# A gated product placed right behind each gate, the convolution's steps respread around it, and the last output weights split behind the last gates

## The chip, the cores and the metric

The kernel runs on one core of one Trainium2 chip. A core has five engines that work side by side, each through its own queue of instructions in a fixed order: TensorE (PE, matrix products; PEld is its weight load), VectorE (DVE), ScalarE (ACT), GpSimd (POOL) and SyncE (SP, which here only issues transfers). They wait for each other through semaphores. Data lies in the on-chip memory SBUF, products come out in PSUM, and everything else is in the device's main memory. The metric is the device time of one execution in microseconds (us), lower is better.

## The reference, cut to what matters

Two layers over 1024 latent tokens of 1024 channels. The change is in the first, even layer: one input projection feeds a convolution branch (A) and a recurrence branch (B); each is gated by a SiLU, and one output projection joins them.

```python
def even_mixer(h, h0, p):
    z = h @ p["w_in"]
    va, vg, ga, xb, gb = jnp.split(z, [...], axis=-1)
    y_a = conformer_conv(va, vg, p) * jax.nn.silu(ga)
    y_b, hT = rglru_branch(xb, p, h0, True)
    y_b = y_b * jax.nn.silu(gb)
    return jnp.concatenate([y_a, y_b], axis=-1) @ p["w_out"], hT
```

`conformer_conv` is `u = va * sigmoid(vg)`, a convolution over 31 neighbouring tokens for each channel on its own, a layer norm over the channels, and a SiLU. The second layer (a pooling mixer) and a final norm follow.

## The kernel before

Channels lie on the 128 partitions, so 1024 channels are 8 tiles (`KT = 8`) of 128 x 1024 tokens, treated in two halves of 512 tokens. A matrix product in full fp32 accuracy is made of three passes: each operand is split into a high part that TensorE takes as it is and a low part, the rest (`mm3_fixed`, line 565: high times high, high times low, low times high for each of 8 k-tiles, so 24 matmuls for one half and 48 for a tile).

Through most of the even layer the order of every engine's instructions is written by hand: `on` (line 549) issues each instruction behind the last one of its engine. The transfers on SyncE's queue are ordered by the scheduler at build time. What runs around the change:

- *Weights.* `raw_split` (584): ScalarE casts a loaded weight tile to its high part (`wh`), GpSimd subtracts to get the low part (`wl`). There are two buffers each for the raw, high and low tile. `gb_weights(j)` (885) does this for the gate's weights of tile j while j < 8, for the output projection's weights `wob` of tile j - 8 after that.
- *Gates.* `gb_product(j, w)` (891) is the product `h @ w_in` for the gate's tile j. Its two PSUM tiles come from a pool of four. `gb_silu(j)` (901) lets ScalarE apply the SiLU into two SBUF tiles `sb` out of a pool of four, so gate j's tiles wait for those of gate j - 2 to be used up.
- *Gated products.* `gated(n, between)` (1068): for each half, SyncE loads the recurrence's row from main memory (`yr`, two buffers), VectorE multiplies it with the gate (both in SBUF), ScalarE casts the result (`ybh`), GpSimd subtracts (`ybl`). These two are TensorE's operand of k-tile n in the output product. Behind each half stand `between` steps of the convolution.
- *Convolution.* `conv(j)` (617) gives VectorE's work on channel tile j in steps, mostly one multiply-add with its accumulator in PSUM. `fill(n)` (692) issues the next n steps, wherever they stand. `ln_sums` (662) adds a finished tile to the layer norm's sums. One step is longer: `edge_sum` and the sum of even and odd columns (both inputs in SBUF).
- *Output products.* In the loop at 1158, `wob` of tile m is multiplied with all eight `ybh`, `ybl` (48 matmuls). For m = 0 the first seven k-tiles of both halves stand first, then k-tile 7 of the first half, its eviction, k-tile 7 of the second half. `wob_evict` (1098) scales on ScalarE, adds the input on GpSimd and stores. After each m, `gb_weights(KT + m + 2)` prepares the weights after the next, and further steps of the convolution are placed.

Of the kernel before, what the change touches and what calls it, by code (L numbers as in the profile page):

```python
# [20 lines left out]
KT = D // P  # L21
# [35 lines left out]
def body(ctx, tc, xT, ctxT, cc, ccol, modT, modW, win, gw, wout, wu, grp, wg, wo1, small, edge, ident, outT):  # L57
# [24 lines left out]
    def ttile(name):  # L82
        return tpool.tile([P, H], F32, tag="t", name=name)
# [4 lines left out]
    def psum(name):  # L88
        return pm.tile([P, H], F32, tag="mm", name=name)


    def wide(name):
        return pc.tile([P, S], F32, tag="xb", name=name)
# [462 lines left out]
    def act(*args, **kw):  # L556
        return on("act", nc.scalar.activation, *args, **kw)

    def cast(dst, src):
        return on("act", nc.scalar.copy, dst, src)  # L560

    def gp(*args, **kw):
        return on("pool", nc.gpsimd.tensor_tensor, *args, **kw)

    def mm3_fixed(ps, w, xs, cols):
        hi, lo = w
        xh, xl = xs
        for k in range(KT):
            kc = slice(k * P, (k + 1) * P)
            on("pe", nc.tensor.matmul, ps, hi[:, kc], xh[k][:, cols], start=(k == 0), stop=False)  # L570
            on("pe", nc.tensor.matmul, ps, hi[:, kc], xl[k][:, cols], start=False, stop=False)
            on("pe", nc.tensor.matmul, ps, lo[:, kc], xh[k][:, cols], start=False, stop=(k == KT - 1))
            yield

    def all_of(steps):
        for _ in steps:
            pass

    def raw_load(src, name):
        raw = wpool.tile([P, D], F32, tag="wr", name=f"wr_{name}")  # L580
        nc.sync.dma_start(raw, src)
        return raw

    def raw_split(raw, name):
        hi = wpool.tile([P, D], F32R, tag="wh", name=f"wh_{name}")
        lo = wpool.tile([P, D], F32R, tag="wl", name=f"wl_{name}")
        cast(hi, raw)
        gp(out=lo, in0=raw, in1=hi.bitcast(F32), op=sub)
        return hi, lo
# [14 lines left out]
    def vec(f, **kw):  # L604
        return on("vec", f, **kw) if fixed[0] else f(**kw)
# [56 lines left out]
    def ln_sums():  # L662
        for j in range(summed[0], ended[0]):
            for h in range(2):
                first = us[0][:, HALF[h]] if j == 1 else lnacc[h][:, :H]
                vec(nc.vector.tensor_tensor, out=lnacc[h][:, :H], in0=first, in1=us[j][:, HALF[h]], op=add)
        summed[0] = max(summed[0], ended[0])
# [24 lines left out]
    def fill(n):  # L692
        while n > 0:
            try:
                next(going[0])
                n -= 1
            except StopIteration:
                if begun[0] >= whole_[0]:
                    return
                going[0] = conv(begun[0])  # L700
                begun[0] += 1

    with ExitStack() as actx:
# [178 lines left out]
        gws = {}  # L882


        def gb_weights(j):
            src, name = ((win[4 * KT + j], f"gb{j}") if j < KT else
                         (wout[j - KT, 1], f"wob{j - KT}") if j < 2 * KT else
                         (win[2 * KT + (0, KT // 2)[j - 2 * KT]], f"ga{(0, KT // 2)[j - 2 * KT]}"))
            gws[j] = raw_split(raw_load(src, name), name)

        def gb_product(j, w):
            if j == 4:
                gps[j] = (lambda t: [t[:, h] for h in HALF])(wide(f"gb{j}"))
            else:
                gps[j] = [psum(f"gb{j}_{h}") for h in range(2)]
            for h in range(2):
                all_of(mm3_fixed(gps[j][h], w, (hh, hl), HALF[h]))
# [3 lines left out]
        def gb_silu(j):  # L901
            sbs[j] = [ttile(f"sb{j}_{h}") for h in range(2)]
            for h in range(2):
                act(sbs[j][h], gps[j][h], AF.Silu)
# [32 lines left out]
    def d2tile(name, dt=F32):  # L937
        return d2pool.tile([P, S], dt, tag="d2", name=name)
# [5 lines left out]
    def vtile(name):  # L944
        return vpool.tile([P, H], F32, tag="v", name=name)
# [122 lines left out]
    def gated(n, between):  # L1068
        th, tl = d2tile(f"ybh{n}", F32R), d2tile(f"ybl{n}", F32R)
        for h in range(2):  # L1070
            y = vtile(f"yr{n}_{h}")
            nc.sync.dma_start(y, yb_raw[n][:, HALF[h]])
            v = sbs[n][h]
            vec(nc.vector.tensor_tensor, out=v, in0=y, in1=v, op=mult)
            cast(th[:, HALF[h]], v)
            gp(out=tl[:, HALF[h]], in0=v, in1=th[:, HALF[h]].bitcast(F32), op=sub)
            fill(between)
        bh.append(th)
        bl.append(tl)
# [4 lines left out]
    gb_weights(5)  # L1084
    gb_product(5, gws[5])
    gated(1, 3)
    for j in range(3, KT + 1):
        if j < KT:
            gb_silu(j)
        if 3 < j < KT:  # L1090
            gb_weights(j + 2)
        if 3 < j < KT - 2:
            gb_product(j + 2, gws[j + 2])
        gated(j - 1, (0, 0, 4, 5, 5, 5, 3, 0)[j - 1])
        ln_sums()


    def wob_evict(m, h):
# [781 lines left out]
```

## Time and profile before

| what | value |
|---|---|
| time, median of 3 runs (lowest to highest) | 1294.51 us (1293.93 to 1298.01) |
| the profiled execution: its time, its span | 1293.43 us, 1291.6 us |
| PE busy, share of the span | 1263.2 us, 98% |
| DVE | 1134.7 us, 88% |
| ACT | 647.6 us, 50% |
| POOL | 287.5 us, 22% |

The span runs from the first to the last instruction of the profiled execution; its time has 1.8 us around that. In a timeline a row is: start and length in us, engine, line of the kernel, operation, what is written and read by tile names, shape, how many (x), and in brackets the idle time before it with what ended it. Line 553 is the helper behind `on`, so instructions there are told apart by their tiles: `conv` and `u` are the convolution, `sb` the gated product (and the SiLU, on ACT), `ybh`/`ybl` its parts, `wh_`/`wl_` parts of weights, `gb` and `wob` the gate's and the output's products. A group of waits has the total, the number of times and the longest. A matmul's row is 0.39 us long, but the next one starts 0.227 us after it, since they overlap. On VectorE too the next instruction starts a little before the end of a row.

### The profile page before, as it was taken

Reading aid. Unit: us, or ns where it says so; the run is one execution under the profiler, and the core shown is the slowest. Engines: PE = TensorE matmul, PEld = TensorE weight load, DVE = VectorE, ACT = ScalarE, POOL = GpSimd, SP = SyncE. Lnnn points to the kernel's source line nnn. Section 1 sums busy time; section 2 is a strip of 40 time slices with the busy share of each in tenths; the row PEclk is TensorE's granted clock in tenths of the full one; section 3 lists DMA queues with packets and bytes.
Section 4 is the critical chain, followed back from the end, with each engine's and each line's share of the span. In section 5 each row is a group of like instructions: output and inputs, shape, how many; then the busy total and the mean of one; then the engine's idle time right before and its main releaser. Section 6 shows DMA issues by size and latency. Waiting matters only on the chain.

```text
span 1291.6 us, 16081 instructions
## 1 busy us (share of the span) xinstructions
PE 1263.2 (98%) x5804; PEld 1039.1 (80%) x5804; DVE 1134.7 (88%) x1761; ACT 647.6 (50%) x937; POOL 287.5 (22%) x146
## 2 busy tenths in 40 slices
PE   9999999999999999999999999999999999999995
PEld 7788888888888887888887878887877888788784
DVE  6899999999999999969869959998999987987775
ACT  8555566656656533237434347534333334645542
POOL 0003464436453466434200032000000000000002
PEclk9999999999999999999999999999999999999997
DMA  9951121112111234432418565333332334968623
GB/s 366 398 215 49 42 74 42 64 42 74 60 63 57 82 114 138 146 133 82 163 49 289 190 220 153 112 131 139 123 127 85 114 122 134 322 214 283 228 75 130
DMA packets 78783, 182.33 MB, mean 141 GB/s; under 512 B 7664, under 2 KB 23408, under 8 KB 78704
## 3 DMA queue, kind: packets, MB, share of 16 engines
q1 hardware_dynamic: 70256, 177.12, 39.5%
q10 hardware_dynamic: 8448, 4.20, 1.2%
q8 instruction: 45, 0.74, 0.2%
q14 instruction: 34, 0.28, 0.1%
HBM read 137.24 MB, written 44.04 MB: 140 GB/s over the span
## 4 chain that ended last, share of the span: by engine, by line
PE 48%; DVE 31%; DMA 13%; issue 4%; ACT 3%; POOL 1%; SPq 0%; POOLq 0%; DVEq 0%; ACTq 0%
DVE conv L553 7%; PE wob L553 6%; PE vg L553 5%; PE va L553 5%; PE xb L553 4%; PE fold L123 3%; DVE l L553 3%; PE g L553 3%; DVE ws L1417 2%; DMA wr_v<-wfold 2%; DMA yr_t<-y_t 2%; PE ga L553 2%; PE ga L146 2%; PE ga L145 2%; PE ga L144 2%
## 5 line engine op out<-in xcount | busy, mean ns | idle before, releaser
L553 DVE SCALAR_TENSOR_TENSOR conv<-u,sm,conv 128x505 f32<-128x505 f32 (+6 forms) x224 | 153.5, 746 | 1.0
L1699 POOL TENSOR_TENSOR o<-x,rr 128x256 f32<-128x256 f32 (+1 forms) x9 | 8.1, 929 | 454.3 <-ACT rr L1687 451.3
L553 ACT ACTIVATE l<-g,sm 128x512 f32<-128x512 f32 (+1 forms) x96 | 58.6, 618 | 57.8 <-PE g L553 57.0
L103 ACT CAST wq_g<-wr_g 128x512 fp32r<-128x512 f32 x48 | 28.2, 620 | 54.1 <-DMA wr_g<-wg 18.2
L123 PE MATMUL fold<-gh,wh_wu 128*128 128x512 f32 x128 | 51.1, 400 | 1.8 <-ACT wh_wu L103 1.8
L553 POOL TENSOR_TENSOR l<-l,l 128x1280 f32<-128x1280 f32 x16 | 47.1, 2966 | 25.6 <-DVE conv L553 14.1
L553 PE MATMUL wob<-ybl,wh_wob 128*128 128x512 f32 x128 | 50.3, 393 | 2.3 <-POOL ybl L553 2.3
L123 PE MATMUL fold<-gh,wl_wu 128*128 128x512 f32 x128 | 50.2, 395 | 0.5 <-DVE wl_wu L104 0.5
L553 PE MATMUL gb<-h0h,wl_gb 128*128 128x512 f32 x128 | 50.0, 391 | 0.4 <-POOL wl_gb L553 0.4
L123 PE MATMUL fold<-gl,wh_wu 128*128 128x512 f32 x128 | 50.2, 392 | 0.0
L103 ACT CAST wq_v<-wr_v 128x512 fp32r<-128x512 f32 x48 | 28.1, 620 | 44.1 <-DMA wr_v<-wfold 18.5
L553 PE MATMUL va<-h0h,wl_va 128*128 128x512 f32 x128 | 50.0, 390 | 0.1
L553 PE MATMUL vg<-h0h,wl_vg 128*128 128x512 f32 x128 | 50.0, 390 | 0.0
L553 PE MATMUL gb<-h0h,wh_gb 128*128 128x512 f32 x128 | 49.9, 390 | 0.0
L553 PE MATMUL wob<-ybh,wh_wob 128*128 128x512 f32 x128 | 49.9, 390 | 0.0
L553 PE MATMUL gb<-h0l,wh_gb 128*128 128x512 f32 x128 | 49.9, 390 | 0.0
L553 PE MATMUL va<-h0h,wh_va 128*128 128x512 f32 x128 | 49.9, 390 | 0.0
L553 PE MATMUL wob<-ybh,wl_wob 128*128 128x512 f32 x128 | 49.9, 390 | 0.0
L553 PE MATMUL vg<-h0l,wh_vg 128*128 128x512 f32 x128 | 49.9, 390 | 0.0
L553 PE MATMUL va<-h0l,wh_va 128*128 128x512 f32 x128 | 49.9, 390 | 0.0
L553 PE MATMUL vg<-h0h,wh_vg 128*128 128x512 f32 x128 | 49.9, 390 | 0.0
L553 DVE TENSOR_TENSOR_SCAN l<-l,l 128x256 f32<-128x256 f32 (+1 forms) x32 | 48.7, 1522 | 1.1
(593 smaller groups left out, 4290.2 us busy)
## 6 DMA issues: line engine op xcount, KB each, us to landing
wr_wu<-wu SPq DMA_DIRECT2D x16, 512.0 KB, 4.7
modw<-modW SPq DMA_DIRECT2D x16, 512.0 KB, 10.2
x_part<-xp SPq DMA_DIRECT2D x32, 256.0 KB, 2.2
mod<-modT SPq DMA_DIRECT2D x32, 256.0 KB, 3.9
wr_v<-wfold SPq DMA_DIRECT2D x16, 512.0 KB, 4.2
wr_g<-wg SPq DMA_DIRECT2D x16, 512.0 KB, 5.3
wr_wo<-wo SPq DMA_DIRECT2D x16, 512.0 KB, 4.4
yr_t<-y_t SPq DMA_DIRECT2D x16, 512.0 KB, 5.7
```

Source lines behind the costliest of these rows:

```text
L103: return (nc.scalar.copy(hi, src), eng.tensor_tensor(out=lo, in0=src, in1=hi.bitcast(F32), op=sub))
L123: m = nc.tensor.matmul(*args, **kw)
L144: mm(ps, hi[:, kc], xh[k][:, cols], start=(k == 0), stop=False)
L145: mm(ps, hi[:, kc], xl[k][:, cols], start=False, stop=False)
L146: mm(ps, lo[:, kc], xh[k][:, cols], start=False, stop=(k == ks - 1))
L553: last[eng] = f(*args, **kw)
L1417: nc.vector.tensor_tensor(out=nxt[:, :, a_:b_], in0=cur[:, :, a_ + o0 : b_ + o0], in1=cur[:, :, a_ + o1 : b_ + o1], op=add)
L1699: nc.gpsimd.tensor_tensor(out=o[:, k - k0], in0=v, in1=rr, op=mult)
```

## The change

Before, the loop for j issues the SiLU of gate j and then the gated product of gate j - 1, so each product stands one gate behind. After, the product of gate j follows the SiLU of gate j. The weights of the gates' tile 6 and the output weights are placed anew between them, and the numbers of convolution steps between the products are others: behind each half of gates 2 to 7 it was 4, 5, 5, 5, 3, 0, and is 2, 3, 5, 5, 5, 4. The weights of output product 1 (`gb_weights(KT + 1)`), which stood ahead of gate 6's product, come behind gate 7's.

```diff
     gb_weights(5)
     gb_product(5, gws[5])
     gated(1, 3)
-    for j in range(3, KT + 1):
-        if j < KT:
+    gb_silu(3)
+    gb_weights(6)
+    gated(2, 2)
+    gb_silu(4)
+    gb_product(6, gws[6])
+    for j in range(3, KT):
+        if j > 4:
             gb_silu(j)
-        if 3 < j < KT:
-            gb_weights(j + 2)
-        if 3 < j < KT - 2:
-            gb_product(j + 2, gws[j + 2])
-        gated(j - 1, (0, 0, 4, 5, 5, 5, 3, 0)[j - 1])
+        if j == 5:
+            gb_weights(7)
+            gb_product(7, gws[7])
+        elif j == 6:
+            gb_weights(KT)
+        gated(j, (3, 5, 5, 5, 4)[j - 3])
         ln_sums()
+    gb_weights(KT + 1)
```

On each engine the same instructions run in both kernels. TensorE's order is unchanged, and so is every order ahead of gate 2's product and behind the weights of output product 1, but for the two layer-norm sums of the next channel tile, which stand three steps earlier. On ScalarE and GpSimd, between those two points, the parts of the weights and of the gated products follow each other as the lines above say. On SyncE the weights' transfers change places with some of the rows' transfers.

## The prediction

> **What bounds the kernel now.** I read the busy table first, then who TensorE waited for around the changed lines, then the timelines of that stretch engine by engine.
>
> ```profile
> span 1291.6 us, 16081 instructions
> PE 1263.2 (98%) x5804; PEld 1039.1 (80%) x5804; DVE 1134.7 (88%) x1761; ACT 647.6 (50%) x937; POOL 287.5 (22%) x146
> ```
>
> TensorE sets the time: 28 us of the span are left to win in the whole kernel. The waits of PE between 420 and 680 us are two groups (total, times, longest), and the starts of four matmuls put a size to them:
>
> ```profile
> PE wob L553 <- POOL ybl L553: 2.3, 3, 1.6
> PE gb L553 <- POOL wl_gb L553: 0.4, 1, 0.4
> ```
> ```profile
> 473.49 0.39 PE L553 MATMUL gb<-h0h,wh_gb 128*128 128x512 f32 x1
> 485.15 0.39 PE L553 MATMUL gb<-h0h,wh_gb 128*128 128x512 f32 x1
> 496.03 0.39 PE L553 MATMUL wob<-ybh,wh_wob 128*128 128x512 f32 x1
> 510.11 0.40 PE L553 MATMUL wob<-ybh,wh_wob 128*128 128x512 f32 x1
> ```
>
> These are the first matmuls of gate product 6, gate product 7, output product 0 and output product 1, each of 48 matmuls. Product 7 runs clean: 496.03 - 485.15 = 10.88, or 0.227 a matmul. Product 6 takes 11.66 (0.78 lost to its low weights), output product 0 takes 14.08 (3.20 lost to the last gated rows). So the stretch can give back 3.98 us at most, 0.31% of the time. What follows it has no slack for PE to hide in:
>
> ```profile
> 496.00:521.00 25.00, 22.68 (x97) 17.80 (x96) 24.61 (x38) 6.90 (x10) 14.09 (x9) 1.00 0.41 138
> 521.00:587.00 66.00, 66.00 (x292) 54.64 (x291) 53.43 (x81) 22.13 (x32) 29.39 (x17) 1.00 0.39 133
> 587.00:677.00 90.00, 90.00 (x398) 74.54 (x398) 71.97 (x110) 48.62 (x74) 19.80 (x9) 1.00 0.30 99
> ```
>
> The second number of a row is PE's busy time: 66.00 of 66.00 and 90.00 of 90.00. When output product 1 starts later by some time, so does everything behind it, up to 677 us and, as the later chain starts from PE's products there, beyond.
>
> **The change part by part.** TensorE's own instruction order is the same in both kernels, and nothing is added or removed on any engine; only orders on VectorE, ScalarE, GpSimd and SyncE change, all between gate 2's product and output product 1. What decides is when the last gated product (gate 7, second half) ends on VectorE, and what GpSimd still has to do before output product 1.
>
> *The end of the chain.* Before, it runs so:
>
> ```profile
> 505.51 1.29 DVE L553 TENSOR_TENSOR sb<-yr,sb 128x512 f32<-128x512 f32 x2
> ```
> ```profile
> 470.97 1.04 ACT L553 CAST wh_gb<-wr_gb 128x1024 fp32r<-128x1024 f32 x1
> 506.23 1.23 ACT L553 CAST ybh<-sb 128x512 fp32r<-128x512 f32 x2 [4.67 <-DVE sb L553]
> ```
> ```profile
> 497.96 2.40 POOL L553 TENSOR_TENSOR wl_wob<-wr_wob,wh_wob 128x1024 fp32r<-128x1024 f32 x1 [2.41 <-ACT wh_wob L553]
> 506.93 2.54 POOL L553 TENSOR_TENSOR ybl<-sb,ybh 128x512 fp32r<-128x512 f32 x2 [3.66 <-ACT ybh L553]
> ```
>
> Call the end of the last gated product X: 505.51 + 1.29 = 506.80. The low part ends at 506.93 + 2.54 = 509.47 (it queues behind its sister half), and output product 1 starts at 510.11, X + 3.31. Its own low weights were made at 497.96, long before. After, `gb_weights(KT + 1)` stands behind the last gated row, so on ScalarE the weights' cast (1.04) follows the last cast, hidden by GpSimd's low part, and on GpSimd the 2.40 follow that low part. The two halves no longer stand back to back, so the low part ends at X + 0.62 + 1.29 + 0.1 of handing over = X + 2.0, the weights at X + 4.4. Output product 1 needs them at its third matmul, 0.45 after its start, and pays about 0.15 of slow first matmuls; that equals a start at X + 4.15. Against X + 3.31: **+0.85**. There is no cover for it, since PE has nothing else in its queue.
>
> *How X moves, the transfer.* Up to the last gated product VectorE has the same work in both orders, counted from gate 2's first half: 44 convolution steps, the two sums for the layer norm, the gated products. So X moves only by waits.
>
> ```profile
> 461.72 1.23 DVE L553 TENSOR_TENSOR sb<-yr,sb 128x512 f32<-128x512 f32 x1
> 462.87 2.71 DVE L553 SCALAR_TENSOR_TENSOR conv<-u,wsum,conv 128x509 f32<-128x509 f32 x4
> 466.76 1.65 DVE L553 TENSOR_TENSOR sb<-yr,sb 128x512 f32<-128x512 f32 x1 [1.18 <-DMA yr<-yb_raw]
> ```
> ```profile
> 462.42 0.33 SPq L581 DMA_DIRECT2D wr_gb<-win  x1
> 462.85 9.13 SPq L1072 DMA_DIRECT2D yr<-yb_raw  x4
> ```
>
> Gate 2's second half waits for its recurrence row, which SyncE issues behind gate 7's weights (512 KB); those wait for GpSimd to finish the low weights of gate 5. Both orders have the two transfers in this sequence, so the row lands at 466.7 again. The new order puts 2 steps instead of 4 (0.655 each, 2.71 for 4 overlapped) before that product: VectorE waits 1.18 + 1.31. **+1.3**; the steps it would have filled the time with come later, before X. Bounds: 0 if the row lands sooner, and +1.3 is also the most that two steps can be.
>
> *How X moves, the meetings with GpSimd.* A VectorE instruction with both inputs in SBUF takes longer when GpSimd is in an instruction of its own. Undisturbed lengths are the first three rows, the others are disturbed:
>
> ```profile
> 450.24 0.68 DVE L553 TENSOR_TENSOR sb<-yr,sb 128x512 f32<-128x512 f32 x1
> 453.69 0.15 DVE L553 SCALAR_TENSOR_TENSOR edge_junk<-u,sm 128x8 f32<-128x8 f32 x1
> 453.89 0.70 DVE L553 TENSOR_TENSOR u<-u 128x512 f32<-128x512 f32 x1
> ...
> 475.27 1.02 DVE L553 TENSOR_TENSOR sb<-yr,sb 128x512 f32<-128x512 f32 x1
> 484.55 0.87 DVE L553 TENSOR_TENSOR sb<-yr,sb 128x512 f32<-128x512 f32 x1
> 499.53 1.38 DVE L553 TENSOR_TENSOR sb<-yr,sb 128x512 f32<-128x512 f32 x1
> 500.83 1.22 DVE L553 SCALAR_TENSOR_TENSOR edge_junk<-u,sm 128x8 f32<-128x8 f32 x1
> 502.10 1.73 DVE L553 TENSOR_TENSOR u<-u 128x512 f32<-128x512 f32 x1
> ```
> ```profile
> 459.99 2.41 POOL L553 TENSOR_TENSOR wl_gb<-wr_gb,wh_gb 128x1024 fp32r<-128x1024 f32 x1 [1.70 <-ACT wh_gb L553]
> 466.58 1.28 POOL L553 TENSOR_TENSOR ybl<-sb,ybh 128x512 fp32r<-128x512 f32 x1 [1.22 <-ACT ybh L553]
> 480.02 3.59 POOL L553 TENSOR_TENSOR wl_gb<-wr_gb,wh_gb 128x1024 fp32r<-128x1024 f32 x1 [1.70 <-ACT wh_gb L553]
> ```
>
> The product at 461.72 ends when GpSimd's at 459.99 does (462.40) plus its own length, the one at 466.76 when the one at 466.58 does; at 480.02 GpSimd was the one to wait (3.59 for 2.40). Before, VectorE loses 0.55 + 0.97 + 0.34 + 0.19 + 0.70 + 1.07 + 1.03 = 4.9. For the new order I walked the queues from 461.72 on with these lengths. Gate 6's low weights now run right behind gate 1's low parts, 467.0 to 469.7: no wait for PE at 473.9, so the 0.78 is gone. But gate 3's first product comes at 468.7 and waits 0.9, its second 0.4, gate 4's first 0.75 behind gate 3's low part. Gate 7's weights now stand behind both rows of gate 4: 483.5 to 485.9. There the two layer-norm sums (484.2) wait 1.7, and PE waits about 1.1 for them (it wants them at 484.8). Output product 0's weights run 494.1 to 496.5, gate 6's first product waits 1.5; the sum of even and odd columns waits 1.0 once more, gate 2's first product its 0.55. That is 6.8: **+1.9**. Bounds: with no new meetings only 0.55 + 1.0 are left, -3.3; with three meetings of a full 2.40 and four of 1.29, 12.4, +7.5. I take the walk's value, as the same walk with the old order ends on X within 0.3 us of the trace.
>
> PE's new wait of 1.1 at gate 7 and the vanished waits cost and bring nothing by themselves: PE meets the chain of X again inside output product 0. That product would start near 496.5, reach the last rows' second half (46th matmul) near 507.5, and stand there some 3 us.
>
> *Sum:* 0.85 + 1.3 + 1.9 = +4.05, with X near 510.0 and output product 1 effectively at 514.15. The profiled execution took 1293.43 (span 1291.6 and 1.8 around it); it becomes 1297.5. The median of the runs, 1294.51, stands 1.08 above that execution, so the forecast is **1298.6**. The later convolution is covered:
>
> ```profile
> DVE ml_mu L553 <- ACT mh_mu L553: 10.0, 1, 10.0
> ```
>
> VectorE idles 10.0 there, ahead of the layer norm's mean, since ScalarE's part of it follows PE's products, which now come 4 later themselves; VectorE comes 3.2 later and still waits. Without this cover PE's mean matmuls would be late by what VectorE is.
>
> **The clock.** The granted clock stays 1.00 over the stretch (the windows' column before the last two) with a PE wait of 1.6 in it (the longest of the `wob` group). If it halved behind the wait of 3 us, each matmul would take 0.227 more; between no matmul and one whole product that is 0 to +10.9. I take 0, as the wait of 1.6 left it whole. The Trainium skill, "TensorE: Matmul & The Clock Gate", "What's actually happening", has the clock halve after an idle window of about 3.4 us and come back after as long a busy one; by it a gap a little longer than mine would cost, as an estimate from that page, 1.7 us more. No gap of the trace of before is long enough to try it.
>
> **The rivals.**
> - *Not slower: the meetings go away.* With products close behind their gates, GpSimd could be done with each low part before VectorE's next product. For it: GpSimd is busy only 14.09 of the 25.00 us of the first window above; against it: the weights' 2.40 now fall into the steps between products three times. Price: -3.3 + 1.3 + 0.85 = -1.15, or 1293.4. It decides once X is below 506.80 - 0.85, i.e. VectorE loses less than 2.8 to meetings. Chance 0.10; only near the ceiling of 3.98 (0.03 of it) would it show as faster by over 0.3%.
> - *The meetings sum up as before.* Then only 0.85 + 1.3 = +2.15 are left: 1296.7. Chance 0.18. A gain of PE elsewhere that takes up part of the shift looks the same from outside.
> - *Slower still.* The weights meet VectorE three times at full length (7.2 of the 12.4 in the bound, so +7.5 less some), or the clock drops behind the long gap: about +7, 1301.5. Chance 0.12.
> - *The change does not do what it says:* a product cannot stand right behind its gate where its row has not landed. For gate 2 that is so, at the +1.3 above, and is in the sum; for the others the rows are issued a whole product ahead (two buffers), so it has no chance of its own.
>
> **How the numbers follow.** The forecast has 0.60, its own range 1297.4 to 1300.6. What a measurement of this kernel can tell from no change is about 0.3%, 3.9 us: slower from 1298.4 on. A sixth of the forecast's chance lies under that, so slower is 0.50 + 0.12 = 0.62; same 0.10 + 0.18 + 0.07 = 0.35; faster 0.03. The range of 8 in 10 leaves out the gain and the top: 1295.2 to 1301.6.
>
> **What would show it.** Right: product 6 without a wait; gate 7's wait for its low weights near 1 us; one PE gap near 3 us late in output product 0, a wait of output product 1 for `wl_wob`, and its successor 4 us later than before; gate 2's second product waiting 2.5 us for its row. Wrong: X at or below 506.8, low weights of output product 1 ready before PE asks, or a lower granted clock; also, PE waits behind 677 us that shrink by the shift.

## The result and the profile after

| | before | after |
|---|---|---|
| time, median of 9 runs (lowest to highest) | 1293.95 us (1293.76 to 1298.01) | 1301.13 us (1298.50 to 1303.51) |
| the profiled execution: time, span | 1293.43, 1291.6 | 1301.71, 1299.9 |

The ratio of after to before is 1.0045, 95% interval 1.0034 to 1.0057: slower by 5.8 us (4.4 to 7.4). The median of after, 1301.13, lies inside the predicted range, 0.5 under its top. The profiled execution of after is the third longest of its nine runs, 8.28 us above that of before.

The busy times of after, and who PE waited for between 420 and 680 us:

```profile
PE 1267.6 (98%) x5804; PEld 1042.0 (80%) x5804; DVE 1137.9 (88%) x1761; ACT 648.4 (50%) x937; POOL 286.0 (22%) x146
```
```profile
PE wob L553 <- ACT ybh L553: 2.2, 1, 2.2
PE gb L553 <- POOL wl_gb L553: 1.8, 1, 1.8
PE wob L553 <- POOL wl_wob L553: 1.1, 1, 1.1
PE wob L553 <- POOL ybl L553: 0.9, 1, 0.9
PE gb L553 <- ACT wh_gb L553: 0.2, 1, 0.2
```

Waits of 6.2 us have taken the place of 2.7, and PE is also *busy* for 4.4 us more (1267.6 against 1263.2) with the same number of matmuls. That is a second effect, which no view of waits shows. The starts of gate product 6 and of output products 0, 1 and 2 in PE's timeline:

```profile
473.37 0.39 PE L553 MATMUL gb<-h0h,wh_gb 128*128 128x512 f32 x1
...
499.25 0.39 PE L553 MATMUL wob<-ybh,wh_wob 128*128 128x512 f32 x1
...
513.74 0.40 PE L553 MATMUL wob<-ybh,wh_wob 128*128 128x512 f32 x1
...
528.78 0.39 PE L553 MATMUL wob<-ybh,wh_wob 128*128 128x512 f32 x1
```

From the first of these to the last is 55.41 us; before it was 521.03 - 473.49 = 47.54. I call this time the *stretch*. It holds 192 matmuls, 43.52 us at 0.227 each, so before had 4.02 to lose and after has lost 7.87 more, nearly the whole 8.28. Gate product 6 runs without a wait now. The engine that sets the end of the chain, VectorE, with GpSimd under it:

```profile
466.71 2.93 DVE L553 TENSOR_TENSOR sb<-yr,sb 128x512 f32<-128x512 f32 x1 [2.75 <-ACT wh_gb L553]
...
470.88 1.71 DVE L553 TENSOR_TENSOR sb<-yr,sb 128x512 f32<-128x512 f32 x1
...
485.12 3.03 DVE L553 TENSOR_TENSOR lnsum<-lnsum,u 128x512 f32<-128x512 f32 x2
...
496.10 2.19 DVE L553 TENSOR_TENSOR sb<-yr,sb 128x512 f32<-128x512 f32 x1
...
506.93 1.80 DVE L553 TENSOR_TENSOR u<-u 128x512 f32<-128x512 f32 x1
...
510.41 0.68 DVE L553 TENSOR_TENSOR sb<-yr,sb 128x512 f32<-128x512 f32 x1
```
```profile
466.70 2.40 POOL L553 TENSOR_TENSOR wl_gb<-wr_gb,wh_gb 128x1024 fp32r<-128x1024 f32 x1 [1.65 <-ACT wh_gb L553]
469.06 2.99 POOL L553 TENSOR_TENSOR ybl<-sb,ybh 128x512 fp32r<-128x512 f32 x2
...
484.65 2.35 POOL L553 TENSOR_TENSOR wl_gb<-wr_gb,wh_gb 128x1024 fp32r<-128x1024 f32 x1 [0.67 <-DMA yr<-yb_raw]
...
495.34 2.40 POOL L553 TENSOR_TENSOR wl_wob<-wr_wob,wh_wob 128x1024 fp32r<-128x1024 f32 x1 [0.68 <-ACT wh_wob L553]
...
506.90 1.29 POOL L553 TENSOR_TENSOR ybl<-sb,ybh 128x512 fp32r<-128x512 f32 x1 [2.69 <-ACT ybh L553]
...
511.83 1.28 POOL L553 TENSOR_TENSOR ybl<-sb,ybh 128x512 fp32r<-128x512 f32 x1 [3.64 <-ACT ybh L553]
513.07 2.38 POOL L553 TENSOR_TENSOR wl_wob<-wr_wob,wh_wob 128x1024 fp32r<-128x1024 f32 x1
```

The products' own length is 0.68. Every long row on VectorE begins inside a row on GpSimd and ends one own length after it, to within 0.2 us: 466.70 + 2.40 + 0.68 gives 469.78 for the first, which ends at 469.64 in the trace. That one is a tie: GpSimd began 0.01 us earlier. X, the end of the last gated product, is 510.41 + 0.68 = 511.09; behind it stand the low part (to 513.11) and the weights of output product 1 (to 515.45), and PE takes the first of them right behind:

```profile
515.50 0.80 PE L553 MATMUL wob<-ybh,wl_wob 128*128 128x512 f32 x1 [1.13 <-POOL wl_wob L553]
516.10 0.63 PE L553 MATMUL wob<-ybh,wh_wob 128*128 128x512 f32 x1
516.52 0.63 PE L553 MATMUL wob<-ybl,wh_wob 128*128 128x512 f32 x1
```

The matmuls behind it start 0.42 after each other, not 0.227.

Windows of 3.41 us of the same execution show where PE's longer busy time comes from (the second number is PE's busy time with its matmuls, the column before the last two the granted clock):

```profile
483.76:487.17 3.41, 1.50 (x6) 0.60 (x6) 3.41 (x4) 0.76 (x1) 2.58 (x2) 1.00 0.06 24
487.17:490.59 3.42, 3.42 (x9) 2.68 (x10) 3.42 (x6) 0.62 (x1) 1.11 (x1) 0.50 0.55 172
490.59:494.00 3.41, 3.41 (x16) 2.81 (x15) 3.38 (x7) 1.34 (x3) 0.81 (x2) 1.00 0.27 76
...
511.07:514.48 3.41, 1.71 (x5) 0.86 (x5) 3.34 (x7) 2.63 (x4) 2.65 (x2) 1.00 0.26 77
514.48:517.90 3.42, 2.40 (x6) 1.94 (x7) 3.42 (x7) 1.15 (x2) 3.42 (x4) 0.50 0.40 101
517.90:521.31 3.41, 3.41 (x10) 2.67 (x9) 3.37 (x7) 0.00 (x0) 2.38 (x2) 0.50 0.66 233
```

The clock is halved in three windows. It drops behind two windows in which PE was busy for 1.50 and 1.71 us, half of the time or less. A fully busy window holds 16 or 17 matmuls at the whole clock, and 9 or 10 in these. The first halving is absorbed, since PE waits for X later anyway, and X does not depend on it: VectorE has no wait between 470 and 512. The other two fall on output product 1, which has nothing to wait for any more. In before the emptiest window of the stretch was followed by no halving:

```profile
500.26:503.67 3.41, 1.82 (x9) 1.33 (x8) 3.38 (x4) 0.62 (x1) 3.02 (x3) 1.00 0.50 150
503.67:507.08 3.41, 3.41 (x17) 2.81 (x16) 3.31 (x7) 0.85 (x2) 0.15 (x1) 1.00 0.20 83
```

### The profile page after: what moved, and what is told of

Read it like the earlier page. It is cut to its first block, busy times and chain, and to the rows that moved or that the text cites. A ratio compares the mean times of both kernels' runs of the same rounds, so it can differ in the third digit from the quotient of the medians.

```text
span 1299.9 us, 16079 instructions
## 1 busy us (share of the span) xinstructions
PE 1267.6 (98%) x5804; PEld 1042.0 (80%) x5804; DVE 1137.9 (88%) x1761; ACT 648.4 (50%) x937; POOL 286.0 (22%) x146
## 4 chain that ended last, share of the span: by engine, by line
PE 54%; DVE 28%; DMA 10%; issue 3%; ACT 2%; POOL 1%; SPq 0%; POOLq 0%; DVEq 0%; ACTq 0%
DVE conv L553 7%; PE wob L553 6%; PE vg L553 5%; PE va L553 5%; PE xb L553 4%; PE fold L123 3%; DVE l L553 3%; PE g L553 3%; DMA yr_t<-y_t 2%; PE ga L145 2%; PE ga L553 2%; PE ga L144 2%; PE ga L146 2%; PE xbc L553 2%; DMA wr_wu<-wu 2%
## 5 line engine op out<-in xcount | busy, mean ns | idle before, releaser
L553 DVE SCALAR_TENSOR_TENSOR conv<-cL,wsum,conv 128x506 f32<-128x506 f32 (+3 forms) x70 | 48.1, 745 | 0.2
```

The costliest lines, as they stand in the source:

```text
L553: last[eng] = f(*args, **kw)
```

## The experiments

The theory after the result was: the chain to X is longer by about what was forecast, and the clock, forecast at nothing, adds the rest. Ratios are to the kernel before, run on the same chip beside each group of kernels: its medians were 1295.36 (e1 to e4), 1295.16 (e0, e5, e6, e8) and 1296.07 (e7, e9, e10). The ratio is from all the runs of a kernel; it is not the quotient of the medians, which differs from it by up to 0.0011 (0.9951 for e9). The stretch is from the one profiled execution of each, which may lie anywhere among its runs: those of e0 and e2 are the shortest, those of e1, e6 and e10 the longest.

| run | edit | stretch | X less start of gate product 6 | clock halved in the stretch | ratio, 95% interval |
|---|---|---|---|---|---|
| before | | 47.54 | 33.31 | none | 1 |
| after | | 55.41 | 37.73 | 10.24 us | 1.0045 (1.0034 to 1.0057) |
| e0 | the changed kernel again | 51.95 | 36.43 | 3.41 | 1.0036 (1.0023 to 1.0049) |
| e3 | after, PE kept busy | 51.40 | 36.40 | none | 1.0028 (1.0017 to 1.0039) |
| e1 | after, output weights early | 53.88 | 38.01 | 10.24 | 1.0060 (1.0046 to 1.0075) |
| e6 | after, gate 2's row first | 53.16 | 36.36 | 6.83 | 1.0032 (1.0020 to 1.0045) |
| e5 | after, gate 7's weights early | 51.87 | 34.93 | 6.83 | 1.0043 (1.0026 to 1.0061) |
| e2 | before, output weights late | 46.06 | 30.41 | none | 0.9999 (0.9986 to 1.0013) |
| e8 | before, fewer steps | 45.93 | 27.16 | none | 0.9998 (0.9985 to 1.0011) |
| e4 | after, fewer steps | 43.61 | 27.95 | none | 0.9966 (0.9947 to 0.9984) |
| e10 | the same once more | 43.60 | 27.91 | none | 0.9968 (0.9957 to 0.9978) |
| e7 | after, three edits | 43.52 | 26.82 | none | 0.9966 (0.9953 to 0.9978) |
| e9 | after, fewer steps, row first | 43.52 | 27.54 | none | 0.9962 (0.9949 to 0.9974) |

**e3: is the clock a cost?** Nineteen matmuls into a PSUM tile that nobody reads stand where PE waits: ten ahead of the last k-tile of output product 0's second half, four ahead of its low part, five ahead of output product 1's low weights.

```diff
+    def busy(n):
+        for _ in range(n):
+            on("pe", nc.tensor.matmul, spin, gws[KT][0][:, 0:P], hh[0][:, HALF[0]], start=True, stop=True)
...
+            if m == 0 and h == 1:
+                busy(10)
+                last_tile(wob_ps[m][h], w, HALF[h], 0)
+                busy(4)
+                last_tile(wob_ps[m][h], w, HALF[h], 1)
+            elif m == 1 and h == 0:
+                steps[h].close()
+                first_tile(wob_ps[m][h], w, HALF[h], 0)
+                busy(5)
+                first_tile(wob_ps[m][h], w, HALF[h], 1)
```

> The changed kernel with 19 more matmuls on TensorE, into PSUM that nobody reads: 10 ahead of the last k-tile of output product 0's second half, 4 ahead of its low part, 5 ahead of output product 1's low weights, so in the three waits of 2.2, 0.9 and 1.1 us. If the clock at half from 514.5 to 521.3 us follows from TensorE standing idle, it stays at 1.00 there, and the time falls by about half of those 6.8 us, 3.4, to 1297.7, though the three waits end no sooner; the half clock at 487 us, ahead of which nothing is filled in, stays. Rival: the half clock has another cause, or did not delay what sets the time; then the time stays at 1301.1 or rises by what the matmuls overrun the waits, under 1 us.

Measured: 1298.64 us (1297.23 to 1301.34, 6 runs), 1.0028. Windows of its profile over the same place:

```profile
505.92:509.33 3.41, 2.71 (x13) 2.02 (x12) 3.31 (x5) 0.00 (x0) 0.92 (x1) 1.00 0.20 73
509.33:512.75 3.42, 2.87 (x12) 1.81 (x11) 3.35 (x7) 2.25 (x4) 2.27 (x2) 1.00 0.22 77
512.75:516.16 3.41, 3.36 (x16) 2.45 (x15) 3.41 (x6) 1.65 (x2) 3.41 (x3) 1.00 0.23 55
```

None of these windows has less than 2.7 of PE's time, and the clock stays whole. The chain ends where it does in e0 (36.40 and 36.43 behind gate product 6); with the clock whole the stretch is 3.86 above before, and the ratio is 3.6 us. So the clock's part is a cost in the profile, and idle work took it away there. How much it is varies: 0.55 us of the stretch against e0, 4.0 against the profile of after, of which the tie has 1.3. The times alone would not show it, since the interval of e3 overlaps those of e0 and of after. One expectation failed: the half clock at gate product 7, for which nothing had been put in, did not come. From one matmul's start to the next, PE's gap there was 1.27 us this time and 2.15 in after.

**e0: how much does the changed kernel scatter?** No edit.

> The changed kernel once more, for the scatter of its runs (1298.5 to 1303.5) and beside the next kernels on one chip. In its first profile gate 2's second product and gate 6's low weights came up within 0.02 us of each other (466.71 and 466.70), and the product took 2.93 us instead of 0.68. If that is a tie, a second profile may show the product first (0.68, and the last gated product about 1 to 1.5 us earlier); and the half clock behind output product 0's waits should come and go in steps of 3.4 us from run to run. If neither varies, the scatter has another source.

Measured: 1299.74 us (1297.08 to 1304.07, 12 runs). Its profile is that of the shortest run, with VectorE, GpSimd's low part of gate 6's weights, and windows so:

```profile
466.57 0.69 DVE L553 TENSOR_TENSOR sb<-yr,sb 128x512 f32<-128x512 f32 x1 [2.60 <-DMA yr<-yb_raw]
...
468.50 1.59 DVE L553 TENSOR_TENSOR sb<-yr,sb 128x512 f32<-128x512 f32 x1
...
471.97 1.08 DVE L553 TENSOR_TENSOR sb<-yr,sb 128x512 f32<-128x512 f32 x1
...
475.25 1.55 DVE L553 TENSOR_TENSOR sb<-yr,sb 128x512 f32<-128x512 f32 x1
```
```profile
466.71 2.82 POOL L553 TENSOR_TENSOR wl_gb<-wr_gb,wh_gb 128x1024 fp32r<-128x1024 f32 x1 [1.65 <-ACT wh_gb L553]
```
```profile
505.26:508.67 3.41, 1.78 (x7) 0.85 (x5) 3.27 (x7) 0.30 (x1) 1.27 (x1) 1.00 0.25 77
508.67:512.08 3.41, 0.69 (x2) 0.38 (x3) 3.34 (x7) 2.15 (x3) 1.52 (x2) 1.00 0.27 77
512.08:515.49 3.41, 3.00 (x7) 1.90 (x7) 3.41 (x7) 1.62 (x2) 3.41 (x3) 0.50 0.08 12
```

Here VectorE was 0.14 us ahead and won the tie (0.69 in place of 2.93), GpSimd waited (2.82 for 2.40), and X stands 1.30 nearer to gate product 6 than in after. Gate product 7 waited 0.9 in place of 1.8, and no window was halved behind it; the waits around X fell on the windows in another way, and one window was halved in place of two. The mean granted clock of the twelve runs goes from 0.994 in this one down to 0.990 in the two of 1303.46 and 1304.07. A share of the scatter can be the number of windows that were halved; the other runs have no profile that would show it. It is not the only source: the kernel before, run beside this one, spread as far (1290.65 to 1298.79 in 27 runs) with a mean clock of 0.992 to 0.995.

**e1: is the late splitting of the output weights worth +0.85?** The weights of output product 1 go ahead of gate 7's product again.

```diff
-        elif j == 6:
-            gb_weights(KT)
+        elif j > 5:
+            gb_weights(j + 2)
...
-    gb_weights(KT + 1)
```

> The changed kernel with the weights of output product 1 put back ahead of gate 7's product. By the prediction's term for them, output product 1 no longer waits for wl_wob (1.1 us in the changed kernel's profile) and the time falls by 0.85 or more, from 1301.1 to about 1300.2. Rival: on GpSimd the 2.40 us of these weights then fall on VectorE's way to gate 7's first product, which waits for them; the last gated product ends 1 to 2 us later, and the time stays within 0.5 us of the changed kernel.

Measured: 1302.97 us (1300.27 to 1304.97, 5 runs), 1.0060. VectorE's row of gate 7's first half and GpSimd's row under it:

```profile
504.51 2.33 DVE L553 TENSOR_TENSOR sb<-yr,sb 128x512 f32<-128x512 f32 x1
```
```profile
503.90 2.39 POOL L553 TENSOR_TENSOR wl_wob<-wr_wob,wh_wob 128x1024 fp32r<-128x1024 f32 x1 [0.67 <-ACT wh_wob L553]
```

Output product 1 no longer waits for its weights, but the weights now meet a gated product (2.33 in place of 0.68), and X is 1.6 later than in e0. For X the rival is borne out: the 2.40 of GpSimd cost no less there than behind the chain. The time is higher than either side had it; the profile, of the longest of the five runs, has three windows halved.

**e2: the splitting alone, in the old order.**

```diff
-        if 3 < j < KT:
+        if 3 < j < KT - 1:
             gb_weights(j + 2)
...
+    gb_weights(KT + 1)
```

> The kernel before, with one thing of the change: the weights of output product 1 behind the last gated product. By the prediction's term it is 0.85 us slower than before, 1294.8. Rival: GpSimd is then free when VectorE comes to gate 6's second half, whose 1.38 us shrink to 0.68, and so are the instructions behind it; the last gated product ends 2 to 3 us earlier than 506.8, and the time falls by about 1 us, to 1292.8.

Measured: 1296.28 us (1291.14 to 1298.18, 12 runs), 0.9999. VectorE's rows of gate 6's second half and the column sum, and GpSimd's weights:

```profile
499.25 0.69 DVE L553 TENSOR_TENSOR sb<-yr,sb 128x512 f32<-128x512 f32 x1
...
500.06 0.69 DVE L553 TENSOR_TENSOR u<-u 128x512 f32<-128x512 f32 x1
```
```profile
506.37 2.38 POOL L553 TENSOR_TENSOR wl_wob<-wr_wob,wh_wob 128x1024 fp32r<-128x1024 f32 x1
```

These two rows had 1.38 and 1.73 in before. With the weights out of the way X is 2.9 earlier against gate product 6; PE then waits 1.1 for the weights, and the stretch is 1.48 shorter. A stretch shorter by 1.48 would be a ratio of 0.9989; the interval holds that and no change, so the time alone decides nothing here.

**e6: is gate 2's wait for its row worth +1.3?** The row's transfer goes ahead of gate 7's weights on SyncE's queue.

```diff
+            with ExitStack() as rctx:
+                if j == 7:
+                    rctx.enter_context(tc.issue_after(rows_in[2, 1].ins))
+                raw = raw_load(src, name)
+            gws[j] = raw_split(raw, name)
...
+            rows_in[n, h] = nc.sync.dma_start(y, yb_raw[n][:, HALF[h]])
```

> The changed kernel with one pair of transfers swapped on SyncE's queue: the row of gate 2's second half ahead of gate 7's weights. By the prediction's term (1.3, of a wait of 2.5 to 2.75) the wait of VectorE goes and the time falls by 1.3 at least, to under 1299.8. Rival: VectorE only comes sooner to meetings with GpSimd (gate 1's low parts, then gate 6's low weights), the last gated product moves by less than 0.5 us, and so does the time.

Measured: 1299.15 us (1297.43 to 1303.04, 8 runs), 1.0032. VectorE's rows of gate 2's second half and gate 3's first:

```profile
464.22 1.72 DVE L553 TENSOR_TENSOR sb<-yr,sb 128x512 f32<-128x512 f32 x1
...
467.18 2.80 DVE L553 TENSOR_TENSOR sb<-yr,sb 128x512 f32<-128x512 f32 x1
```

The wait of 2.60 is gone, and X is where it was (36.36 against 36.43): the two products come earlier, into GpSimd's low parts and gate 6's weights, and lose there what the wait had cost. The rival is borne out. The time does lie under the 1299.8 named, but so does that of the changed kernel beside it (1299.74), and the ratios differ by 0.0004.

**e5: gate 7's low weights one gate earlier,** so that neither PE nor the layer norm's sums stand behind them.

```diff
-        if j == 5:
+        if j == 4:
             gb_weights(7)
+        elif j == 5:
             gb_product(7, gws[7])
```

> The changed kernel with gate 7's weights placed ahead of gate 4's products instead of behind them. If GpSimd's low weights in the way of the two layer-norm sums cost what the prediction's walk says (1.7 us on VectorE, 1.1 on TensorE at gate product 7), gate product 7 finds its weights ready, the two sums are back at 1.28 us together, the last gated product ends about 1.5 us earlier, and the time falls by as much, to 1299.6. Rival: the weights meet gate 4's products there instead, and the time is the changed kernel's within 0.5.

Measured: 1299.82 us (1297.99 to 1305.59, 8 runs), 1.0043. VectorE's row of the two sums:

```profile
484.10 1.28 DVE L553 TENSOR_TENSOR lnsum<-lnsum,u 128x512 f32<-128x512 f32 x2
```

They took 3.03 in after. X moved by -1.5 against e0, and gate product 7 has no wait, as the theory wants; yet the stretch is the same (51.87 against 51.95). PE's gap of 3.23, start to start, late in output product 0 begins earlier too, at 505.8 in place of 507.3, but two windows were halved behind it, 510.18 to 517.01, where e0 had one. The time shows no gain, and the interval is too wide to show 1.5 us either way. Whether an execution with another position of the windows would have kept the gain was not tried.

**e4, e10: fewer steps ahead of X.** If X is what PE waits for, steps of the convolution taken from ahead of it must bring PE's time back whichever order is used; 34 in place of 44 stand there.

```diff
-    gated(2, 2)
+    gated(2, 3)
...
-        gated(j, (3, 5, 5, 5, 4)[j - 3])
+        gated(j, (2, 3, 5, 4, 0)[j - 3])
```

> The changed kernel with fewer convolution steps between the gated products (behind each half of gates 2 to 7: 3, 2, 3, 5, 4, 0 instead of 2, 3, 5, 5, 5, 4, so 34 instead of 44 ahead of the last product); the others follow later. If the end of the last gated product sets the time, it comes some 10 us earlier than in the changed kernel, TensorE meets it without a wait and at full clock, output product 2 starts 3 to 4 us earlier than before, and the time is about 1290.3. Rival: the steps pushed back are missed at the layer norm, where VectorE had 10.0 us to spare, or a later wait takes the gain: 1294 or more.

> The changed kernel with fewer steps (34 in place of 44 ahead of the last gated product) once more. Theory: 0.9966 of before again, within 0.002, with output product 2 at 517.5 and no PE wait over 0.5 in the stretch. Rival (the gain was the scatter of this chip's runs): 0.999 to 1.001.

Measured: 1292.07 us (1288.68 to 1293.37, 6 runs), 0.9966, and again 1291.86 us (1289.44 to 1296.09, 12 runs), 0.9968: faster than both kernels. One window of the first over the stretch:

```profile
473.50:517.50 44.00, 44.00 (x196) 36.27 (x195) 43.54 (x63) 14.85 (x24) 27.97 (x17) 1.00 0.39 132
```

PE is busy for 44.00 of 44.00: of the 4.02 that before lost, all but 0.1 are back. VectorE is as full as ever (43.54); the steps it leaves out here it does later, and PE does not miss them: its products for the layer norm's mean start 48.96 behind output product 2, as in before, though VectorE's wait ahead of the mean is down to 2.5.

**e8: the same number of steps in the old order.** Is it the order or the number?

```diff
-        gated(j - 1, (0, 0, 4, 5, 5, 5, 3, 0)[j - 1])
+        gated(j - 1, (0, 0, 3, 4, 4, 4, 2, 0)[j - 1])
```

> The kernel before, its order kept, with 34 convolution steps instead of 44 ahead of the last gated product (3, 4, 4, 4, 2, 0 behind each half of gates 2 to 7). If only the end of the last gated product counts, it is as fast as the changed order with 34 steps (0.9966 of before). If the changed order has a worth of its own once the steps are out of the way, this one is slower than that: gate product 6 still waits for its low weights, gate 6's product still stands behind output product 1's weights, and the gain is about 1.4 us, 0.999 of before.

Measured: 1294.20 us (1291.71 to 1298.67, 12 runs), 0.9998. X comes as early as in e4, but the stretch is 45.93. The same window, VectorE's last row, and GpSimd's rows at that time:

```profile
473.50:517.50 44.00, 42.18 (x185) 34.30 (x184) 42.85 (x64) 14.49 (x22) 28.22 (x18) 1.00 0.42 137
```
```profile
498.04 2.53 DVE L553 TENSOR_TENSOR sb<-yr,sb 128x512 f32<-128x512 f32 x1 [0.77 <-ACT ybh L553]
```
```profile
497.62 2.40 POOL L553 TENSOR_TENSOR wl_wob<-wr_wob,wh_wob 128x1024 fp32r<-128x1024 f32 x1 [5.25 <-ACT wh_wob L553]
499.98 5.48 POOL L553 TENSOR_TENSOR ybl<-sb,ybh 128x512 fp32r<-128x512 f32 x4
```

In the old order the last rows follow each other closely and meet the weights of output product 1, and output product 0 reaches for gate 6's low part (first of the four) before it is there: PE waits 1.6 for it. So the changed order, the late weights included, is worth something once the steps are out of its way: 43.61 against 45.93, and intervals of the ratio that do not overlap. Which part of it is open. The low part that PE waits for stands behind the weights on GpSimd, and with the late weights of e2 that wait was gone, so e2's edit on top of this one might bring as much; the old order with 34 steps and the late weights was not run.

**e7 and e9: the repairs together.** e7 has the edits of e4, e5 and e6, e9 those of e4 and e6.

> The changed kernel with three edits at once: steps 3, 2, 3, 5, 4, 0 behind the halves of gates 2 to 7 (34 in place of 44), gate 7's weights ahead of gate 4's gated products, gate 2's second-half row ahead of gate 7's weights. Theory (the end of the chain moves by the work and the waits ahead of it, and the clock stays whole when PE has no waits): last gated product ends near 500, no PE wait over 0.5 between gate product 6 and output product 2, which starts near 517.0, as in the kernel with fewer steps alone (517.46), clock 1.00 over the stretch; ratio 0.996 to 0.998 of before. Rival (the steps missed here delay PE later, where VectorE's convolution ends): output product 2 just as early, but new PE waits behind 560, ratio 0.999 to 1.001.

> The changed kernel with steps 3, 2, 3, 5, 4, 0 and gate 2's second-half row ahead of gate 7's weights. Theory (wait for the row and meetings take each other's place): output product 2 near 517 to 517.5, as with fewer steps alone (517.46), ratio 0.996 to 0.998 of before. Rival (the row is a term of its own): one more us won, output product 2 near 516.4, and not to be had, since PE has no wait left there; a ratio below 0.996 would speak for it.

Measured: 1291.19 us (1288.61 to 1292.61, 5 runs), 0.9966, and 1289.76 us (1289.12 to 1292.91, 5 runs), 0.9962. In the window from 473.50 to 517.50 PE of e9 is busy for 44.00 of 44.00. The stretch is 43.52 in both, the bare 192 matmuls. Nothing is left in it to win, so these two cannot be told from e4, as theory had it for the row; the rival of e7, new waits further on that take the gain back, is not seen in the time. Of the three edits the fewer steps alone are thus enough.

## Why the prediction was right, and where it was off

*What bounds the kernel.* Right. In all thirteen profiles PE's first product of the second layer (675 us in before) starts 154.2 us behind output product 2, so a shift of the stretch is carried whole that far. Behind it the rest of the span takes 615.8 to 623.2 us, in no order of the stretch (616.4 in before, 616.9 in after, 622.9 in e10): a scatter that shows no link to the change, and that hides a us or two in single executions. Over many runs the ratio goes with the stretch: 0.9962 to 0.9968 at 43.5 to 43.6, 0.9998 and 0.9999 at 45.9 and 46.1, 1.0028 to 1.0060 from 51.4 on. VectorE was covered as said; its wait ahead of the layer norm's mean was 10.3 in e0, 7.7 in e3 and 13.4 in after, against 10.0. The ceiling of the gain, 3.98, is what e4, e7 and e9 show (3.93 to 4.02).

*X, +3.2 forecast (1.3 and 1.9).* Right as a sum: X less the start of gate product 6 rose by 3.12 in e0 and 3.09 in e3. The meetings came where the walk put them: in e0 0.91, 0.40 and 0.87 at gates 3 and 4 (forecast 0.9, 0.4 and 0.75), then, as in the rows of after above, 1.7 at the layer norm's sums (3.03 for 1.28), 1.5 at gate 6 and 1.1 at the column sum. The walk called gate 2's wait a term of its own, and that was wrong: e6 took the wait away, and X stayed. Wait and meetings exchange, since GpSimd's low parts and weights stand where they did (gate 6's weights end at 469.4 in e6, 469.5 in e0). Nor did the walk see the tie, which cost the profiled execution of after 1.3 more (4.42 in place of 3.12).

*Output product 1's weights, +0.85.* Right in size: from X to output product 2 were 14.23 before and 15.00 in e3, +0.77. But it isn't a price of the late place alone, as e1 showed: the early place costs 1.6 at X.

*No cost at gate product 6, a wait near 1 at gate product 7, one near 3 late in output product 0, one for `wl_wob`.* All four are there, and so is the wait of gate 2's second product (2.75, and 2.60 in e0). Gate product 7 waited 0.9 in e0 and 1.8 in after, where the tie had pushed its weights back.

*The sum, +4.05.* With the clock whole (e3) the stretch grew by 3.86 and the time by 3.6. The step that was mis-sized is the last: "I take 0, as the wait of 1.6 left it whole". The clock was halved for 3.41 to 10.24 us of the stretch, a sign that the prediction itself had put down as one of being wrong. From X to output product 2, with the weights in the same place, were 15.00 in e3, 15.52 in e0 and 17.68 in after: the halved windows cost 0.5 and 2.7 there. With the tie (0 and 1.3) the stretch grew by 4.41 and 7.87 in these two, and the measured 5.8 (4.4 to 7.4) lies between; that clock and tie make up the whole difference from 4.05 is argued from these two profiles.

The argument looked at the longest wait and not at how full PE's windows were. PE was busy for 1.82 of the 3.41 us of the emptiest window of the stretch in before, and a window with 1.71 was followed by a halving in after. And it overlooked an example at the end of before's own trace, in the final norm, where two waits of 1.36 and 2.03 us, with four short matmuls between, were followed by the half clock, though neither is as long as a window:

```profile
1275.08:1278.49 3.41, 0.61 (x4) 0.52 (x4) 3.41 (x6) 0.68 (x2) 3.17 (x3) 1.00 0.41 154
1278.49:1281.90 3.41, 2.92 (x8) 1.85 (x8) 3.15 (x10) 0.63 (x2) 0.70 (x2) 0.50 1.01 371
```

The bound of 0 to +10.9 held the cost, and so did the range; that was in part luck, since the time lies 0.5 under the top of the range and above 1300.6, where the forecast's own range ended.

*The rivals.* "Slower still" named the clock as one of its two causes and lies nearest to the time of after; "the meetings sum up as before" fell, with 6.9 lost to them in e0 against 4.9; "the meetings go away" fell in this kernel, but e2 shows the meetings at the end of the old order going away when the weights are moved, at 1.48 of the stretch.

## What to carry to other kernels

Where one engine (here VectorE) feeds the bound one through a chain, look first at what work without a deadline stands ahead of the chain's end: ten convolution steps moved back took 8.3 us off the stretch in the changed order (51.95 to 43.61) and 1.6 in the old one, while the edits of single waits gained nothing: e1 and e6 exchanged one cost for another, and what e5 won at X was lost again in the clock. Two waits of PE that come close together can cost more than their sum, so one should ask of each stall which share of a clock window it empties, not only how long it is. A change of order and a change of the amount of work between should be tried apart: the changed order was the better one with 34 steps, and the 44 around it hid that.

## What the runs showed of the hardware

The clock's windows lie on a fixed grid within an execution, and not behind PE's waits. In after the second halving begins 514.48 - 487.17 = 27.31 us behind the first, 8 times 3.41; in e5 halvings begin at 510.18, 721.80 and 817.38, which is 62 and 90 times 3.413 behind the first; in e6 two are 209 times 3.413 apart. Cut along this grid, the thirteen profiles have some 4800 windows at the whole clock. The next one was halved behind all 17 in which PE was busy for less than 1.5 us, behind 7 of 13 between 1.5 and 1.9, and behind none of the others. Between 1.5 and 1.9 the busy time alone does not decide: 1.85 was followed by a halving in e6, 1.71 was not in e8. So a stall of 2.15 us, start to start, can halve the clock if it lies in one window (483.76 to 487.17 in after, 1.50 busy), and one of 3.23 with its neighbours was followed by one halved window in e0 and by two in e5 and e6. Where the grid falls differs between executions; so the same stall can cost more or less from one execution to the next. The Trainium skill, "TensorE: Matmul & The Clock Gate", "What's actually happening", has this window as free-running and 3413 ns long, and the trace agrees. It has the clock halve after an idle window; here a window that was half busy was enough.

A VectorE instruction with both inputs in SBUF and one of GpSimd's subtractions here do not run side by side: the one that starts second ends about one own length behind the first. A tenth of a us decides which of them waits. In after GpSimd was 0.01 us ahead and the product took 2.93; in e0 VectorE was 0.14 ahead, the product took 0.69 and GpSimd 2.82 for 2.40. The Trainium skill, "SBUF — State Buffer", "Who interferes with whom", says that a VectorE instruction with two inputs in SBUF contends with a GpSimd instruction that reads SBUF, and that the order of issue decides who blocks; these rows agree.
